# Stick-breaking and MoBA scores as two float32r products, a first stage of seven PSUM banks fed one block at a time, and a planner with leads by stage

## The chip, the cores and the metric

The kernel runs on one core of a Trainium2 chip. The metric is the device time of one launch in microseconds. Before the change it is 1304.44 us, the median of three runs (1304.07 to 1304.82).

## The reference

Two stacks of two layers each over 256 tokens of width 1024 (batch 1). A layer of the first stack computes a modulation vector from `c` (`silu(c) @ w_ada + b_ada`), normalises and modulates x, and multiplies by a wide `w_in` whose columns are split:

```python
hdn = modulate(rmsnorm(x, norm1_g[l]), shift1, scale1)
proj = hdn @ w_in[l]
q_lat, c_kv, k_pe, sb_qkv, mb_qkv, gates = jnp.split(proj, SPLIT_POINTS, axis=-1)
```

Three attentions with 8 heads follow. Multi-head latent attention (MLA) goes through the latents `q_lat` and `c_kv`; its heads have width 96. Stick-breaking attention (heads of width 64) takes a cumulative product of `sigmoid(-score)` in place of a softmax. MoBA (heads of width 64, rotary embedding on 16 columns) is at this length plain causal softmax. The three results are gated, projected, summed and added to x; then comes a squared-ReLU feed-forward of width 4096. A layer of the second stack (the first of them on 512 tokens, 256 of x and 256 of a context; the last on the 256 of x as queries) has softmax attention, a Fourier mixer, a pooling branch and a short convolution, each gated by a `silu` of its own columns and concatenated before an output projection.

## The kernel before, in words

The program is written as a recording. `record` (from line 499) runs the whole computation once against an object that notes every operation with its engine, its buffers and a modelled cost (`Recorder.cost`). `Scheduler` then orders the operations: `forward` places them greedily by priority on five engines, with a limited number of buffers (`SLOTS` and `CAPS`: 40 SBUF tiles of 128x1024, 11 of 128x544, and 8 PSUM banks in two classes, four "mm" and four "tr"); `backward` gives each operation its latest time, from which the next pass's priority is made after subtracting a lead. `LEAD` names a lead for eight kinds of work (`nc.part`), and the best of `PASSES` = 8 passes is kept. `emit` (line 447) issues the operations in that order, so every instruction of the profile carries the line of the one call in `emit`, L463. Tiles are told apart by their names.

Nearly all matrix products are products of float32r parts: an operand is split into a rounded part (`hi`, a cast on ScalarE) and the rest (`lo`, a subtraction on VectorE), and `mm3` (line 529) issues three matmuls, hi by hi, hi by lo and lo by hi. `wload` loads a weight tile and splits it (`raw`, `whi`, `wlo` in the profile). `gemm_tok` puts tokens on the PSUM partitions, `gemm_col` puts output columns there ("g" and "gc"). In the second stack, "cb" are the column products of the branches and `store_cat` (line 1403) splits each branch result into `cat`, with the subtraction on GpSimd.

The beginning is `lat_first` (line 1044). It loads x, normalises and transposes it ("nT_n"), and then goes in four steps of two blocks of 128 input rows: `ada_lead` loads the part of `w_ada` for the shift and scale of those two blocks (eight multiply-adds of 512 columns on VectorE, "acc"; then four one-column matmuls, "mT"), two normalised blocks are modulated and split into `hT0h` and `hT0l`, and 1312 columns of `w_in` are multiplied: the 1056 of the latents ("lat", six banks of 352 columns) and the first 256 of the stick-breaking queries ("latq"). Two of the three `lo` parts of the latents' weights are made on GpSimd.

The rest of `w_ada` and all of `w_mod_2` is multiplied by vectors on VectorE between other work: a generator (`filler`) hands out a quarter of a chunk at a time, at `RATE` per megabyte of weights loaded, or all at once when the result is needed.

Scores of stick-breaking and MoBA attention are plain float32 products in `causal_attention` (line 971). `to_q` (line 1038) copies the transposed queries into one of two tiles, `q_pad`, in which the other head's 64 partitions are zero, so that a product over 128 partitions with a `kT` tile that holds two heads gives one head's scores. For each attention and layer there are 16 such products, 8 with 128 key columns and 8 with 256 ("s_sb", "s_mb"). A float32 product appears in the trace as two matmul instructions.

```python
for i, h in enumerate(heads):
    mm(ps[:, i * nk:(i + 1) * nk], qT(h)[:, t * 128:(t + 1) * 128], kT(h)[:, 0:nk],
       start=(i == 0), stop=True)
```

Of the kernel before, what the change touches and what calls it, by code (L numbers as in the profile page):

```python
# [167 lines left out]
class Recorder:  # L168
    ENGINES = ("tensor", "vector", "scalar", "gpsimd", "sync")

    def __init__(self):
        self.protos = bacc.Bacc("TRN2", target_bir_lowering=False, num_devices=1)
        self.ops = []
        self.bufs = []
        self.masks = {}
        self.part = None
        self.group = None
        self.proto_of = {}
        for e in self.ENGINES:
            setattr(self, e, Engine(self, e))  # L180
# [311 lines left out]

VEC = (("norm1_g", 8), ("norm2_g", 8), ("b_ada", 48), ("q_norm_g", 6), ("kv_norm_g", 2),
# [3 lines left out]
def record(nc, a, out):  # L497
# [46 lines left out]
    vt = fixed([128, 24 + L * vn], F32, "vt")  # L544
    nc.sync.dma_start(out=vt, in_=a["vecs"])
    nc.sync.dma_start(out=ct[:, 0:128], in_=a["const_early"][:, 0:128])
    for t in range(2):
        nc.sync.dma_start(out=x[:, t], in_=a["x"][0, t * 128:(t + 1) * 128, :])
    x_late = nc.ops[-1]
    nc.sync.dma_start(out=ct[:, 128:cn], in_=a["const_early"][:, 128:cn])  # L550
    nc.order(x_late, nc.ops[-1])
# [11 lines left out]
    nc.vector.tensor_tensor(cT, vt[:, 0:24], cT, op=ALU.mult)  # L563

# [7 lines left out]
    def rope_tables():  # L572

        nc.sync.dma_start(out=pos_i, in_=a["positions"].rearrange("o (t p) -> p (o t)", p=128),
# [19 lines left out]

    rope_tables()
# [37 lines left out]
    def ada_raw(w2d, k, per, c0, count, n, name):  # L633
# [3 lines left out]
        for i in range(count):  # L637
            src = w2d[k * 128:(k + per) * 128, c0 + i * D:c0 + i * D + n]
            nc.sync.dma_start(out=view[:, :, i], in_=src.rearrange("(k p) n -> p k n", p=128))
            if first_weights:  # L640
                nc.order(first_weights[0], nc.ops[-1])
# [9 lines left out]
    def ada_chunk(w2d, c0, count, accs):  # L651
# [11 lines left out]
        for (_, fin), acc in zip(accs, tiles):  # L663
            fin(acc)
        yield

    def row_sum(acc, name):

        p = TR(f"rs{name}")
        with nc.together(87.0):  # L670
            for i in range(4):
                mm(p[32 * i:32 * i + 32, 0:256], ones_f, acc[:, i * 256:(i + 1) * 256])
        row = S2(f"rr{name}", 256)
        nc.scalar.copy(row, p[:, 0:256])
        turn = T([4, 256], F32, "dram", f"turn{name}")
        nc.sync.dma_start(out=turn, in_=row[0:128:32, :])
        return turn

    def ada_lead(w2d, key, bias, j):

        uid[0] += 1
        u = uid[0]
        acc = S2(f"acc{u}", 512)
        p = TR(f"mT{u}")
        for k in range(0, 8, 2):
            raw = ada_raw(w2d, k, 2, j * 256, 2, 256, f"araw{u}_{k}")
            for i in range(2):
                mul_add(acc, raw[:, i], 0, k + i)
        for b in range(4):
            mm(p[:, b:b + 1], acc[:, b * 128:(b + 1) * 128], ones_f[:, 0:1], start=(b == 0), stop=True)  # L690
        o = 2 * j
        nc.vector.tensor_tensor(modT[key].rearrange("p (i b) -> p i b", i=2)[:, :, o:o + 2],
                                p[:, 0:4].rearrange("p (i b) -> p i b", i=2),
                                bias.rearrange("p (i b) -> p i b", i=2)[:, :, o:o + 2], op=ALU.add)

    def fin_T(key, bias, q):

        def f(acc):
            nm = f"{uid[0]}_{key[0]}"
            turn = row_sum(acc, nm)  # L700
# [6 lines left out]
        return f  # L707

    def fin_bc(key, bias_row):

        def f(acc):
# [4 lines left out]
            turn = row_sum(acc, f"{uid[0]}_{key[0]}g")  # L716
            nc.sync.dma_start(out=g, in_=turn.rearrange("a n -> (a n)").partition_broadcast(128))
        return f
# [35 lines left out]
    def filler_step():  # L754
        try:
            next(filler[0][1])
        except StopIteration:
            filler.pop(0)

# [211 lines left out]
    def causal_attention(qT, kT, vf, scale, mask, act, name, rows, table=None):  # L971

        def probs(t, heads):
# [4 lines left out]
            for i, h in enumerate(heads):  # L978
                mm(ps[:, i * nk:(i + 1) * nk], qT(h)[:, t * 128:(t + 1) * 128], kT(h)[:, 0:nk],
                   start=(i == 0), stop=True)  # L980
# [51 lines left out]


    q_pad = [fixed([128, 4, 256], F32, f"q_pad{r}") for r in range(2)]
    for r in range(2):
        nc.gpsimd.memset(q_pad[r][64 - 64 * r:128 - 64 * r], 0.0)

    def to_q(b, p):

        for r in range(2):  # L1040
            nc.scalar.copy(q_pad[r][64 * r:64 * r + 64, b:b + 2], p[64 * r:64 * r + 64])


    def lat_first(w_in, g, act, evac, q0, q_evac):


        xT = [S4(f"xT{t}").rearrange("p (k t) -> p k t", k=8) for t in range(2)]
        for t in range(2):
            rr = rstd(sq_all(x[:, t], f"x0{t}"), D, f"n10{t}", EPS)
            xn = S4(f"xn_n10{t}")  # L1050
            nc.vector.tensor_scalar(xn, x[:, t], rr, math.sqrt(D), op0=ALU.mult, op1=ALU.mult)
            for k0 in (0, 4):
                p = TR(f"nT_n10{t}{k0}")
                for k in range(4):
                    nc.tensor.transpose(p[:, k * 128:(k + 1) * 128], xn[:, (k0 + k) * 128:(k0 + k + 1) * 128], ident)
                nc.scalar.copy(xT[t][:, k0:k0 + 4], p.rearrange("p (k t) -> p k t", k=4))
        key = ("a", 0, 0)
        modT[key] = fixed([128, 16], F32, "modT_a00")
        A = small(8, "A_n10")
        ps = {(t, c): (MM if c < 2 else TR)(f"lat{t}{c}") for c in range(3) for t in range(2)}  # L1060
        pq = TR("latq")
        last = None
        for k in range(0, 8, 2):
            i0 = len(nc.ops)
            nc.part = "lead"
            ada_lead(a["w_ada"][0], key, vec(0, "b_ada")[:, 0:16], k // 2)
            if last is not None:
                nc.order(last, next(op for op in nc.ops[i0:] if op.eng == "sync"))
            nc.vector.scalar_tensor_tensor(A[:, k:k + 2], modT[key][:, 8 + k:10 + k], 1.0, g[:, k:k + 2],
                                           op0=ALU.add, op1=ALU.mult)  # L1070
            for t in range(2):
                nt = S2(f"nt_n10{t}{k}", 256).rearrange("p (k t) -> p k t", k=2)
                for i in range(2):
                    nc.scalar.activation(nt[:, i], xT[t][:, k + i], AF.Identity, scale=A[:, k + i:k + i + 1],
                                         bias=modT[key][:, k + i:k + i + 1])
                for _, _, h, lo in act.spans(k, 2):
                    hv, lv = h[:, :, tok(t)], lo[:, :, tok(t)]
                    nc.scalar.copy(hv, nt)
                    nc.vector.tensor_tensor(lv, nt, hv.bitcast(F32), op=ALU.subtract)
            nc.part = None  # L1080
            i0 = len(nc.ops)
            ws = [wload(w_in, k * 128, 2, c * 352, 352, None if c == 0 else nc.gpsimd) for c in range(3)]
            wq = wload(w_in, k * 128, 2, q0, 256)
            last = [op for op in nc.ops[i0:] if op.eng == "sync" and op.bufs[0].kind == "r"][-1]
            for t in range(2):
                for c in range(3):
                    for i, (wh, wl) in enumerate(ws[c]):
# [633 lines left out]
```

## Time and profile before

| what | value |
|---|---|
| median of three runs | 1304.44 us |
| the profiled execution's own time | 1304.07 us |
| its span (first to last instruction) | 1302.3 us |
| mean granted TensorE clock | 0.997 of full |
| matmuls on TensorE | 1269.2 us busy, 97% |
| VectorE | 1027.5 us busy, 79% |
| ScalarE | 709.5 us busy, 54% |
| GpSimd | 135.5 us busy, 10% |
| moved by DMA | 272.67 MB, 209 GB/s over the span |

Matmuls are pipelined: one that is listed with 280 ns may start 118 ns after the one before. What a matmul costs TensorE is therefore read from the distance of two starts, not from its duration. A busy share of 97% does not say that nothing waits. The profile starts its clock at the first instruction, and the own time of an execution is 1.8 us longer than its span.

### The profile page before, as it was taken

How to read it: one execution, taken by the hardware profiler on the slowest of the kernel's cores; microseconds unless marked ns; L12 is line 12 of the kernel's file. 1: busy time of each engine (PE TensorE's matmuls, PEld its weight loads, DVE VectorE, ACT ScalarE, POOL GpSimd, SP SyncE). 2: the span in 40 equal slices, each digit the busy share in tenths (PEclk: the TensorE clock that was granted, in tenths of full speed). 3: DMA queues.
4: the chain of work that ended last, by engine and by line, in shares of the span. 5: the costliest groups of instructions: out<-in, count | busy, mean ns of one | idle time of the engine just before them, and what ended most of it. 6: DMA issues, size and time to landing. Idle time of an engine off the chain costs nothing.

```text
span 1302.3 us, 21802 instructions
## 1 busy us (share of the span) xinstructions
PE 1269.2 (97%) x8228; PEld 1119.8 (86%) x8228; DVE 1027.5 (79%) x1619; ACT 709.5 (54%) x1224; POOL 135.5 (10%) x142
## 2 busy tenths in 40 slices
PE   5999999999999999999999999999999999999998
PEld 4999989998898989999899988898878776788886
DVE  6898878977876667878687879987978868968874
ACT  5667656644655536566565545656555443326551
POOL 3300000110000000200000110000001033601232
PEclk9999999999999999999999999999999999999999
DMA  9987575665888667775755756897662326716530
GB/s 313 353 282 241 157 265 178 227 196 181 290 300 294 213 192 258 238 258 169 248 174 176 260 202 215 254 319 230 200 221 78 121 68 220 223 40 209 162 116 33
DMA packets 168031, 272.67 MB, mean 209 GB/s; under 512 B 26139, under 2 KB 65007, under 8 KB 167926
## 3 DMA queue, kind: packets, MB, share of 16 engines
q1 hardware_dynamic: 167926, 271.28, 62.8%
q8 instruction: 64, 1.05, 0.3%
q14 instruction: 41, 0.34, 0.1%
HBM read 270.11 MB, written 1.13 MB: 208 GB/s over the span
## 4 chain that ended last, share of the span: by engine, by line
PE 53%; DMA 3%; DVE 2%; issue 1%; ACT 1%; POOL 1%; SPq 0%; DVEq 0%; ACTq 0%; POOLq 0%
PE g L463 11%; PE gc L463 9%; PE cb L463 8%; PE ff L463 7%; PE f L463 7%; PE qkvp L463 2%; DMA raw<-w_in 1%; PE ufp L463 1%; POOL mean L463 1%; PE s_l L463 1%; PE pT_l L463 1%; PE pv L463 1%; PE s_ml L463 0%; PE s_mb L463 0%; DMA araw<-w_ada 0%
## 5 line engine op out<-in xcount | busy, mean ns | idle before, releaser
L463 ACT CAST whi<-raw 128x1024 fp32r<-128x1024 f32 (+3 forms) x370 | 368.8, 1012 | 254.3 <-DMA raw<-w_ff 66.2
L463 DVE TENSOR_TENSOR wlo<-raw,whi 128x1024 fp32r<-128x1024 f32 (+3 forms) x362 | 425.4, 1199 | 64.8 <-ACT whi L463 48.6
L463 DVE SCALAR_TENSOR_TENSOR acc<-araw,cT,acc 128x1024 f32<-128x1024 f32 (+1 forms) x175 | 211.6, 1226 | 23.0 <-DMA araw<-w_ada 18.2
L463 PE MATMUL gc<-hT1h,whi 128*128 128x256 f32 x256 | 78.8, 308 | 0.0
L463 PE MATMUL gc<-hT0h,whi 128*128 128x256 f32 x240 | 74.0, 308 | 0.0
L463 PE MATMUL gc<-hT1l,whi 128*128 128x256 f32 x256 | 72.0, 281 | 0.0
L463 PE MATMUL gc<-hT1h,wlo 128*128 128x256 f32 x256 | 72.0, 281 | 0.0
L463 PE MATMUL gc<-hT0h,wlo 128*128 128x256 f32 x240 | 67.5, 281 | 0.0
L463 PE MATMUL gc<-hT0l,whi 128*128 128x256 f32 x240 | 67.3, 281 | 0.0
L463 PE MATMUL f<-fT1h,whi 128*128 128x256 f32 x192 | 54.3, 283 | 0.0
L463 PE MATMUL f<-fT0h,whi 128*128 128x256 f32 x192 | 54.0, 281 | 0.0
L463 PE MATMUL f<-fT1l,whi 128*128 128x256 f32 x192 | 53.9, 281 | 0.0
L463 PE MATMUL f<-fT1h,wlo 128*128 128x256 f32 x192 | 53.9, 281 | 0.0
L463 PE MATMUL f<-fT0h,wlo 128*128 128x256 f32 x192 | 53.8, 280 | 0.0
L463 PE MATMUL f<-fT0l,whi 128*128 128x256 f32 x192 | 53.8, 280 | 0.0
L463 PE MATMUL cb<-h20h,whi 128*128 128x512 f32 x128 | 53.3, 417 | 0.0
L463 PE MATMUL cb<-h20h,wlo 128*128 128x512 f32 x128 | 51.0, 399 | 0.0
L463 PE MATMUL cb<-h20l,whi 128*128 128x512 f32 x128 | 51.0, 398 | 0.0
L463 PEld LDWEIGHTS gc<-hT1h,whi 128*128 128x128 f32 x256 | 48.3, 189 | 2.1 <-issue 1.3
L463 PEld LDWEIGHTS gc<-hT1l,whi 128*128 128x128 f32 x256 | 48.5, 190 | 0.5
L463 PEld LDWEIGHTS gc<-hT1h,wlo 128*128 128x128 f32 x256 | 48.4, 189 | 0.0
L463 PEld LDWEIGHTS gc<-hT0h,whi 128*128 128x128 f32 x240 | 45.3, 189 | 2.7 <-issue 2.1
(639 smaller groups left out, 3720.0 us busy)
## 6 DMA issues: line engine op xcount, KB each, us to landing
raw<-w_in SPq DMA_DIRECT2D x138, 512.0 KB, 4.9
raw<-w_ff SPq DMA_DIRECT2D x128, 512.0 KB, 5.1
araw<-w_ada SPq DMA_DIRECT2D x128, 256.0 KB, 4.8
araw<-w_ada SPq DMA_DIRECT2D x32, 512.0 KB, 4.4
raw<-w_out SPq DMA_DIRECT2D x32, 512.0 KB, 5.3
araw<-w_mod SPq DMA_DIRECT2D x64, 256.0 KB, 4.6
raw<-w_in SPq DMA_DIRECT2D x24, 352.0 KB, 6.5
araw<-w_mod SPq DMA_DIRECT2D x16, 512.0 KB, 5.4
```

The source lines that it names most:

```text
L463: op.inst.append(getattr(getattr(nc, op.eng), fn)(*[val(x) for x in args], **{k: val(x) for k, x in kw.items()}))
```

## The change: what it does

It has several parts.

- Scores: queries and keys of stick-breaking and MoBA are kept as float32r. A tile of queries holds a head's rounded part on its own 64 partitions and the rest on the other 64; the tile of keys holds the rounded keys on both halves, and a second tile `k_low` the rest of the keys on the head's half and zeros on the other. Two products over 128 partitions give hi by hi plus lo by hi, and hi by lo. MLA scores stay float32.
- First stage: `lead_first` takes the place of `lat_first`. It goes block by block (eight steps of 128 input rows), with `w_ada` and `w_in` columns laid out for it ahead of the launch, and fills seven banks of 512: the 512 query, 512 key and 512 value columns of stick-breaking and 256 gate columns, 1792 in all. For the first two blocks the modulation is multiplied on TensorE (32-column stationary tiles, "c_col"), for the other six on VectorE in pieces of 256 columns. The latents come afterwards by `gemm_tok`. All `lo` parts of its weights are made on VectorE. Rotary tables are made after it, and the order of the first loads changes.
- Filler: where one chunk serves two vectors (second stack), the sums of both go through one bank and one copy.
- `kpe` (MLA): one transpose of a padded tile in place of two. Pool branch: the matmuls of both halves are issued together.
- `store_cat`: the subtraction moves from GpSimd to VectorE.
- Planner: a lead for each of some 35 stages is added to the lead by kind, the leads by kind are changed, `PASSES` is 3 in place of 8 and `RATE` 0.4354 in place of 0.428.

```diff
-            op.lead = 0.0 if eng == "sync" else LEAD.get(self.part, 0.0)
+            op.lead = 0.0 if eng == "sync" else LEAD.get(self.part, 0.0) + LEAD.get(self.stage, 0.0)
...
-    q_pad = [fixed([128, 4, 256], F32, f"q_pad{r}") for r in range(2)]
+    k_low = [fixed([128, 4, 256], F32R, f"k_low{r}") for r in range(2)]
...
+        def to_q(self, b, p):
+            for r in range(2):
+                own, other = (slice(64 * i, 64 * i + 64) for i in (r, 1 - r))
+                hi = self.q[r][own, b:b + 2]
+                nc.scalar.copy(hi, p[own])
+                nc.vector.tensor_tensor(self.q[r][other, b:b + 2], p[own], hi.bitcast(F32), op=ALU.subtract)
+
+        def to_k(self, b, p):
+            for r in range(2):
+                own, other = (slice(64 * i, 64 * i + 64) for i in (r, 1 - r))
+                hi = self.k[r][own, b:b + 2]
+                nc.scalar.copy(hi, p[own])
+                nc.vector.tensor_tensor(k_low[r][own, b:b + 2], p[own], hi.bitcast(F32), op=ALU.subtract)
+                nc.scalar.copy(self.k[r][other, b:b + 2], p[own])
+
+        def scores(self, o, h, t, nk, first):
+            q, r = self.q[h % 2][:, h // 2, t * 128:(t + 1) * 128], h % 2
+            mm(o, q, self.k[r][:, h // 2, 0:nk], start=first, stop=False)
+            mm(o, q, k_low[r][:, h // 2, 0:nk], start=False)
...
+        for k in range(8):
+            nc.part = "lead"
+            acc = S2(f"acc_l{k}", 256)
...
+            raws = [load(a["lead_ada"][k, :, i * 1024:(i + 1) * 1024], 1024, f"araw_l{k}{i}") for i in range(2)]
...
+            if k < LEAD_ROWS:
+                r = TR(f"mR_l{k}")
+                for i in range(2):
+                    with nc.together(87.0):
+                        for q in range(4):
+                            mm(r[32 * q:32 * q + 32, 0:256], c_col[:, 4 * i + q], raws[i][:, q * 256:(q + 1) * 256],
+                               start=(i == 0), stop=(i == 1))
+                nc.scalar.copy(acc, r[:, 0:256])
+            else:
+                for q in range(8):
+                    mul_add(acc, raws[q // 4][:, (q % 4) * 256:(q % 4 + 1) * 256], 0, q)
...
+            nt = S2(f"nt_n10{k}", 256)
+            for o in (act.h(k), nt):
+                nc.scalar.activation(o, xT[k // 4][:, k % 4], AF.Identity, scale=A[:, k:k + 1], bias=mod[:, 0, k:k + 1])
+            nc.vector.tensor_tensor(act.l(k), nt, act.h(k).bitcast(F32), op=ALU.subtract)
...
+                nc.scalar.copy(hi[:, 0:n], raw)
+                nc.vector.tensor_tensor(lo[:, 0:n], raw, hi[:, 0:n].bitcast(F32), op=ALU.subtract)
...
+            lead_first(vec(0, "norm1_g"), hT,
+                       [(0, "col", put_q(0)), (256, "col", put_q(1)), (512, "col", put_k(0)), (768, "col", put_k(1)),
+                        (1536, "col", lambda p: nc.scalar.activation(gt_lead[:, 0:512], p, AF.Tanh, scale=0.5)),
+                        (1024, 0, put_v(0)), (1024, 1, put_v(1))])
+            rope_tables()
...
-            nc.gpsimd.tensor_tensor(cat.l(kb)[:, sl], c, h.bitcast(F32), op=ALU.subtract)
+            nc.vector.tensor_tensor(cat.l(kb)[:, sl], c, h.bitcast(F32), op=ALU.subtract)
...
-PASSES = 8
-RATE = 0.428
-LEAD = {"norm": 2550.0, "lead": 2700.0, "residual": -2030.0, "sb": -4670.0, "ml": -11260.0, "mb": -7380.0,
-        "attention2": -8540.0}
+PASSES = 3
+RATE = 0.4354
+LEAD = {"norm": 2550.0, "lead": 2700.0, "lead weights": 2950.0, "residual": -1660.0, "sb": -8810.0, "ml": -16600.0,
+        "mb": -6240.0, "attention2": -17800.0, "ada": 3060.0, "att mb0": -190.0, "att mb1": -1340.0,
...
```

## Rows read from the trace of the kernel before

**Rows 1.** The page: TensorE's and VectorE's busy time; the chain's shares by engine.

```profile
PE 1269.2 (97%) x8228; PEld 1119.8 (86%) x8228; DVE 1027.5 (79%) x1619; ACT 709.5 (54%) x1224; POOL 135.5 (10%) x142
...
PE 53%; DMA 3%; DVE 2%; issue 1%; ACT 1%; POOL 1%; SPq 0%; DVEq 0%; ACTq 0%; POOLq 0%
```

**Rows 2.** Windows of 50 us: busy of each engine, clock, DMA share, GB/s.

```profile
0.00:50.00 50.00, 32.84 (x180) 30.14 (x181) 36.78 (x57) 24.57 (x47) 17.38 (x21) 0.97 0.97 316
...
800.00:850.00 50.00, 50.00 (x331) 44.64 (x330) 48.72 (x47) 27.89 (x35) 0.00 (x0) 1.00 0.85 274
...
1050.00:1100.00 50.00, 47.58 (x257) 34.72 (x256) 37.78 (x65) 18.61 (x47) 18.29 (x19) 0.97 0.41 136
...
1200.00:1250.00 50.00, 47.18 (x363) 42.52 (x363) 41.59 (x78) 26.48 (x49) 12.64 (x17) 1.00 0.47 154
1250.00:1300.00 50.00, 46.98 (x304) 38.70 (x302) 29.31 (x52) 17.12 (x37) 12.98 (x14) 1.00 0.21 70
sum 1300.00, PE 1269.17 PEld 1119.76 DVE 1027.53 ACT 709.46 POOL 135.52; mean PE 48.81 PEld 43.07 DVE 39.52 ACT 27.29 POOL 5.21
```

**Rows 3.** Timeline of TensorE in the first stage: start, duration, what, count.

```profile
19.27 0.66 PE L463 MATMUL lat<-whi,hT0h 128*128 128x352 f32 x1 [0.42 <-ACT hT0h L463]
...
48.35 1.02 PE L463 MATMUL mT<-ones_f,acc 128*128 128x1 f32 x8
...
58.65 0.28 PE L463 MATMUL latq<-hT0h,whi 128*128 128x256 f32 x1
58.76 0.28 PE L463 MATMUL latq<-hT0l,whi 128*128 128x256 f32 x1
...
60.08 0.28 PE L463 MATMUL gc<-hT0h,whi 128*128 128x256 f32 x1
```

**Rows 4.** Groups of VectorE instructions by form, mostly to 60 us: count, busy, mean ns.

```profile
L463 DVE SCALAR_TENSOR_TENSOR acc<-araw,cT,acc 128x512 f32<-128x512 f32 x28 | 22.3, 798 | 0.8
L463 DVE TENSOR_TENSOR hT0l<-nt_n,hT0h 128x256 fp32r<-128x256 f32 x8 | 4.0, 516 | 0.7 <-ACT hT0h L463 0.6
L463 DVE TENSOR_TENSOR wlo<-raw,whi 128x1024 fp32r<-128x1024 f32 x3 | 3.7, 1223 | 1.0 <-PE lat L463 0.7 <-ACT whi L463 0.3
L463 DVE TENSOR_TENSOR wlo<-raw,whi 128x704 fp32r<-128x704 f32 x4 | 3.5, 878 | 0.0
...
L463 DVE SCALAR_TENSOR_TENSOR A_n<-modT_a,vt 128x2 f32<-128x2 f32 x16 | 4.7, 325 | 0.3
```

**Rows 5.** One tile's instructions (s_mb) and TensorE's timeline around them.

```profile
L463 PE MATMUL s_mb<-kTmb,q_pad x64: 270/326/382, 216.7 to 710.8; 128*128 128x128 f32 x32, 128*128 128x256 f32 x32
...
216.69 0.61 PE L463 MATMUL s_mb<-kTmb,q_pad 128*128 128x128 f32 x4
217.06 0.36 PE L463 MATMUL gc<-hT0h,whi 128*128 128x256 f32 x1
217.26 0.28 PE L463 MATMUL gc<-hT0l,whi 128*128 128x256 f32 x1
...
709.36 0.59 PE L463 MATMUL s_mb<-kTmb,q_pad 128*128 128x256 f32 x2
709.60 0.47 PE L463 MATMUL gc<-oml1h,whi 128*128 128x256 f32 x1
709.90 0.28 PE L463 MATMUL gc<-oml1l,whi 128*128 128x256 f32 x1
```

**Rows 6.** Copies of queries out of PSUM; a VectorE operation that reads PSUM.

```profile
L463 ACT COPY q_pad<-gc x6: 581/582/587, 66.0 to 532.6; 64x512 f32<-64x512 f32 x6
...
L463 DVE TENSOR_TENSOR rt_o<-g,gate_a 128x512 f32<-128x512 f32 x8 | 5.5, 689 | 3.3 <-PE g L463 3.3
```

**Rows 7.** The chain that ended last, near the end: start, length, what.

```profile
1274.48 1.21 POOL cat1l L463
...
1277.63 2.62 POOL cat1l L463 x2
```

**Rows 8.** Timeline at 1076 us, VectorE and TensorE: who waits for what.

```profile
1076.71 1.99 DVE L463 SCALAR_TENSOR_TENSOR acc<-araw,cT,acc 128x1024 f32<-128x1024 f32 x1 [2.29 <-DMA araw<-w_mod]
...
1082.81 0.41 PE L463 MATMUL pT_l<-ct,p_l 128*128 128x128 f32 x2 [1.91 <-DVE p_l L463]
```

More of the change, by code (lines that the diff above doesn't have):

```diff
@@ L176, in __init__ @@
         self.part = None
+        self.stage = None
         self.group = None
@@ L490, in spans @@
             k += m
+LEAD_RANGES = ((1056, 2592), (5152, 5408))
+LEAD_ROWS = 2
+LEAD_COLS = sum(e - s for s, e in LEAD_RANGES)
 VEC = (("norm1_g", 8), ("norm2_g", 8), ("b_ada", 48), ("q_norm_g", 6), ("kv_norm_g", 2),
@@ L544, in record @@
     vt = fixed([128, 24 + L * vn], F32, "vt")
+    nc.sync.dma_start(out=x[:, 0], in_=a["x"][0, 0:128, :])
     nc.sync.dma_start(out=vt, in_=a["vecs"])
     nc.sync.dma_start(out=ct[:, 0:128], in_=a["const_early"][:, 0:128])
[L547 to L551, printed above, removed]
+    nc.sync.dma_start(out=x[:, 1], in_=a["x"][0, 128:256, :])
     pos_i = fixed([128, 2], I32, "pos_i")
@@ L715, in f, with after @@
             nc.vector.tensor_tensor(acc[0:1, :], acc[0:1, :], g[0:1, :], op=ALU.add)
-            turn = row_sum(acc, f"{uid[0]}_{key[0]}g")
-            nc.sync.dma_start(out=g, in_=turn.rearrange("a n -> (a n)").partition_broadcast(128))
-        return f
+        def after(turn):
+            nc.sync.dma_start(out=gate_bc[key], in_=turn.rearrange("a n -> (a n)").partition_broadcast(128))
+        return before, after
     def ada_first(l, part):
@@ L758, in filler_step @@
             filler.pop(0)
+        nc.stage = stage
     def filler_tick(n):
@@ L1057, in lat_first @@
         key = ("a", 0, 0)
         modT[key] = fixed([128, 16], F32, "modT_a00")
+        mod = modT[key].rearrange("p (i b) -> p i b", i=2)
+        bias = vec(0, "b_ada")[:, 0:16].rearrange("p (i b) -> p i b", i=2)
         A = small(8, "A_n10")
[L1060 to L1063, printed above, removed]
-            i0 = len(nc.ops)
[L1065 to L1069, printed above, removed]
-                                           op0=ALU.add, op1=ALU.mult)
[L1071 to L1079, printed above, removed]
-            nc.part = None
[L1081 to L1087, printed above, removed]
-                        mm3(ps[t, c][:, 0:352], act.h(k + i)[:, tok(t)], act.l(k + i)[:, tok(t)], wh, wl,
-                            k + i == 0, k + i == 7)
-            for i, (wh, wl) in enumerate(wq):
-                for m in range(2):
-                    c = slice(m * 128, (m + 1) * 128)
-                    mm3(pq[:, m * 256:(m + 1) * 256], wh[:, c], wl[:, c], act.h(k + i), act.l(k + i),
-                        k + i == 0 and m == 0, k + i == 7)
@@ L1097, in lat_first @@
+        first_weights.extend(last)
         rate[0] = RATE
-        for t in range(2):
-            for c in range(3):
-                evac(t, ps[t, c][:, 0:352], c)
     def first_layer(l, ss1, after_ff):
@@ L1332, in first_layer @@
             ff2(g - 2, hid[g - 2])
+        nc.stage = f"ff end{l}"
         res = after_ff(ss)
@@ L1522, in second_layer @@
             store_cat(m, zf[:, m], p[:, 0:W])
+        nc.stage = f"pool{l}"
         ups = []
```

237 lines of the change are left out of this document (157 added, 80 removed), and 6 rows, old and new, of the table LEAD.

## The prediction, made before the change was run

> **What bounds the kernel now.** I read the page first. TensorE has matmuls in flight for 97% of the span, no other engine reaches 80%, and the chain that ended last is mostly TensorE, with DMA, VectorE, ScalarE, GpSimd and issue time at 8% together, about 104 us [rows 1]. So TensorE is the bound, and a change pays if it takes matmul time away, puts matmuls where TensorE now waits, or removes a wait. Then the windows of 50 us: the idle time over the run is 1300 - 1269.2 = 30.8 us, of which 17.2 lie in the first 50 us; 2.4, 2.8 and 3.0 us lie in the stretches 1050 to 1100 and 1200 to 1300 (the second stack's attention and the end), and only some 5.4 us in everything else [rows 2]. Waits shorter than a matmul's own latency are not in that sum, since pipelined matmuls overlap them. Last, the price of a matmul: two starts of 256 columns of float32r are 0.118 us apart within a run of twelve [rows 3].
>
> The sum is made against the profiled execution's own 1304.1 us, which lies 0.4 us under the median of the runs; I make no correction for that. What a measurement of this kernel can tell from no change is about 0.2%, 2.6 us.
>
> **First stage.** In the kernel before, the first weight matmul starts at 19.3 us and the stage ends at 60.1 us, where the next product follows without a gap [rows 3]. It covers 1312 columns; the new one covers 1792. The 480 columns more are 3.75 groups of 128, times 8 blocks, times 3 matmuls at 0.118 us: 10.6 us of TensorE that no longer follow the stage. What counts is when the new stage ends.
>
> Its loads: x 1.05 MB, constants and vectors 0.2 MB, eight times 1.05 MB of modulation weights and 0.92 MB of projection weights, together 17 MB; at the 316 GB/s of the first 50 us [rows 2] that is 54 us. TensorE needs 7 banks x 6 x 0.118 = 5.0 us a block, 40 us, so it can follow. VectorE is the tighter one. A block from the third on has eight multiply-adds of 256 columns. From the two widths of the weight subtraction a column costs (1223 - 878) / 320 = 1.08 ns, so the 798 ns of 512 columns become 0.52 us at 256 [rows 4]; eight are 4.1 us. To that come the weight subtractions of 1024 and 768 columns, 1.22 and 0.95 us, the activation's, 0.5, and two tiny ones at up to 0.33 us [rows 4]: 7.2 us a block with some overlap, 43 us for six blocks. The third block's first modulation weights land after 5.4 MB, at 17 us. So VectorE is done at 60 us and TensorE, with the last block's seven banks behind it, at 65: 5 us later than now. Net 10.6 - 5.2, I take **-5 us**. Ends: -11 if VectorE is not what limits and the stage ends where it ends now, +4 if each block loses 1 us more to the chain from modulation over ScalarE to TensorE. The two blocks whose modulation goes through TensorE cost it some 2 us while it waits anyway. The rotary tables and the later first loads lie under this stage and cost nothing; without that cover, they would meet the latents' products, which follow.
>
> [...]
>
> **Scores.** Each of two attentions in two layers has 8 products of 128 key columns and 8 of 256, and each float32 product is two instructions [rows 5]. The pair with 256 columns costs 709.90 - 709.36 - 0.118 = 0.42 us, the pair with 128 (217.26 - 216.69 - 0.118) / 2 = 0.23 us [rows 5]. After the change a product is two float32r matmuls. With 256 columns that is 2 x 0.118 = 0.24 us: 32 x 0.19 = 6 us less. No row shows float32r with 128 moving columns. The nearest is a float32 matmul of a single column, 8 in 1.02 us, 0.11 to 0.13 us each [rows 3]: loading 128 stationary columns seems to set a floor. By it two matmuls cost 0.22 us, what the pair costs now, and I take 0 for these. Ends: 0.059 each, half of a 256-column one, gives 3.5 us more; if float32r at 128 columns costs what float32 does, 7 us are lost. **-6 us**, from -9.5 to +1.
>
> [...]
>
> **What the scores need.** A pair of head groups now takes, for queries, two copies on ScalarE and two subtractions on VectorE, and for keys four and two. Over four projections with four evacuations each, that is 24 copies more at 0.58 us on ScalarE, 14 us, and 32 subtractions from PSUM at 0.69 us on VectorE, 22 us [rows 6]. They lie beside TensorE, which has gate and value columns to multiply meanwhile; ScalarE is busy half the time. A PSUM bank is held some 2 us longer at the keys. I cost it at **0**, with an end of +6 where the cover is gone; late next would be the first scores of each attention.
>
> **store_cat.** Near the end the chain goes through GpSimd's subtractions for 1.21 and 2.62 us [rows 7]. On VectorE one of 256 columns is at most 0.52 us [rows 4], two 1.0: **-3 us**, since TensorE's last products stand behind them; from -4 to +2, if VectorE has older work in its queue. In the first layer of the second stack it costs VectorE 6 us that it has there.
>
> **Small ones, 0 together.** The filler's sums have as many matmuls as before, one copy and one bank less where there are two vectors; the transposes of `kpe` are two fewer over the run; the pool matmuls wait for the later of two halves, within 1 us either way.
>
> **Order.** Leads by stage change the order everywhere. The waits of rows 2 outside the first stage are 13.6 us, and those of the second stack come from order: VectorE stands 2.3 us behind a load of filler weights, and TensorE then waits 1.9 us for a softmax row [rows 8]. The filler has its own lead now, and the attention of the second stack a much larger one. I take **-9 us** (8 of visible idle, less the 3 already counted, and 4 of waits inside busy time). The ends are wide, as no row prices an order: -30, under a third of the chain's 104 us, and +12.
>
> Sum: -5 - 6 + 0 - 3 - 9 = -23, so **1281 us**.
>
> **Rivals.** *Order gives much more*: the waits hidden in busy time come out as well, -25 to -30 in place of -9: 1260 to 1265. For it: 104 us of the chain are not TensorE's. Against it: 13.6 us only are visible. *The gains don't arrive*: the new first stage ends 10 us later than the old, so that its columns are paid again, or the order loses about as much as it wins: 1288 to 1300. For it: six blocks of 7.2 us on a VectorE with nothing to spare. *VectorE becomes the bound*, slower: it gets 22 us for the heads, 8 x 0.88 = 7 us of latent weights that GpSimd now has, and 10 us of `store_cat`, 39 us in all. If they all lengthen the way, 1281 + 39 = 1320 us. It decides where VectorE nears 98% of a stretch. Against it: at 800 to 850 us it is busy for 48.7 of 50 us and TensorE does not idle [rows 2], and over the run it has 20% left. *float32r at 128 columns costs as much as float32*: 7 us less gain, 1288.
>
> **Chances.** Forecast (1268 to 1288) 0.42; more from the order (1250 to 1268) 0.27; gains that don't arrive, with the dear 128 columns (1288 to 1302) 0.20; VectorE as the bound or an order that loses more than all the gains (over 1307) 0.08; in between, within 0.2%, 0.03. So faster by over 0.2% is 0.89, within 0.2% 0.03, slower 0.08. The range from 1256 to 1299 leaves out the 0.08 and 0.03 above, and some 0.07 below.
>
> **What would show it.** The first stage: its last matmul at 63 to 68 us, VectorE without gaps from 17 us on, and the latents' products behind it without a wait. Scores: starts 0.118 us apart at 256 columns and about 0.11 at 128; 0.06 or 0.23 there proves the floor wrong. The end: no GpSimd in the last 30 us of the chain. Order: less than 10 us of TensorE idle after the first stage. The forecast is wrong if VectorE's busy share passes 90% over stretches in which TensorE idles, or if the first stage ends after 72 us.

## The result, and the profile after

The changed kernel takes 1312.41 us (1312.01 to 1313.49, 4 runs) against 1304.26 us beside it. The ratio is 1.0068, with a 95% interval of 1.0056 to 1.0080: 0.7% slower. Forecast were 1281 us, in a range from 1256 to 1299.

The profiled execution has a span of 1310.1 us, an own time of 1312.1 us and a mean granted clock of 0.991. The page's busy times, to be held against [rows 1]:

```profile
PE 1270.7 (97%) x8258; PEld 1116.8 (85%) x8258; DVE 1044.5 (80%) x1705; ACT 727.0 (55%) x1246; POOL 85.0 (6%) x112
```

TensorE is in flight as long as before, although the scores are cheaper (a pair of 256 columns takes 0.23 us where it took 0.42, e13 below). The windows tell where the time is. First two wide ones of the kernel before, the second up to its last matmul; its short ones are [rows 2] (columns: busy of TensorE, its weight loads, VectorE, ScalarE and GpSimd, then the granted clock, the DMA share and GB/s):

```profile
0.00:150.00 150.00, 132.20 (x929) 124.61 (x930) 125.63 (x205) 98.11 (x171) 26.18 (x36) 0.99 0.84 280
...
150.00:1298.00 1148.00, 1136.97 (x7301) 995.15 (x7300) 900.52 (x1413) 611.35 (x1054) 109.33 (x106) 1.00 0.61 201
```

The same two of the changed kernel, and then its short ones up to 150 us:

```profile
0.00:150.00 150.00, 127.95 (x876) 116.13 (x877) 116.63 (x231) 98.70 (x169) 8.50 (x28) 0.94 0.73 251
...
150.00:1305.80 1155.80, 1142.71 (x7384) 1000.63 (x7383) 926.51 (x1473) 628.25 (x1078) 76.50 (x84) 1.00 0.61 203
...
0.00:50.00 50.00, 37.49 (x253) 30.46 (x253) 31.48 (x68) 29.42 (x46) 4.86 (x17) 0.97 0.90 311
50.00:100.00 50.00, 43.89 (x269) 41.92 (x267) 40.34 (x79) 36.27 (x70) 1.16 (x2) 0.93 0.80 275
100.00:150.00 50.00, 46.57 (x356) 43.75 (x357) 44.80 (x86) 33.02 (x54) 2.48 (x10) 0.94 0.50 167
```

Two things are to be seen. From 150 us to the last matmul the visible idle time of TensorE is 11.0 us before (1148.0 - 1136.97) and 13.1 after (1155.8 - 1142.71): the new order took none of it away. In the first 150 us it grew from 17.80 to 22.05 us, and the granted clock fell: 0.03, 0.07 and 0.06 of 50 us are 8.0 us of lost clock, 6.5 more than before (0.03 of 50 us there). Another 1.5 us are lost at 1000 to 1050 (granted 0.97), as before at 1050 to 1100 [rows 2].

The place is in TensorE's timeline of the changed kernel (start, duration, what, count; in brackets the idle time before it and who ended it):

```profile
57.72 0.39 PE L464 MATMUL ld<-hT0h,whi_l 128*128 128x256 f32 x1 [1.66 <-ACT hT0h L464]
58.67 0.58 PE L464 MATMUL ld<-hT0l,whi_l 128*128 128x256 f32 x1 [0.57 <-DVE hT0l L464]
...
62.46 0.41 PE L464 MATMUL ld<-hT0h,wlo_l 128*128 128x256 f32 x1
62.68 0.41 PE L464 MATMUL ld<-hT0h,whi_l 128*128 128x256 f32 x1
...
71.77 0.39 PE L464 MATMUL ld<-whi_l,hT0l 128*128 128x512 f32 x1
72.00 0.32 PE L464 MATMUL g<-whi,hT0h 128*128 128x352 f32 x1
...
96.08 0.28 PE L464 MATMUL s_sb<-kssb,qssb 128*128 128x128 f32 x1
96.19 0.28 PE L464 MATMUL s_sb<-k_low,qssb 128*128 128x128 f32 x1
100.04 1.51 PE L464 MATMUL nT_ql<-ct,xn_ql 128*128 128x128 f32 x6 [3.57 <-DVE ssv_ql L464]
102.35 1.47 PE L464 MATMUL nT_kvl<-ct,xn_kvl 128*128 128x128 f32 x4 [0.79 <-DVE nt_ql L464]
103.47 0.67 PE L464 MATMUL g<-whi,laT0h 128*128 128x384 f32 x1
```

The first stage ("ld") ends at 72.0 us, not 65. It waits 2.2 us at 57 to 59, and after that 256-column matmuls start 0.21 us apart (granted clock 0.57 and 0.58 in the windows of the last section, 0.50 in those of 2 us from 60 to 64); from 67 to 70 us, at a granted clock of 1.00, they start 0.118 us apart, as in [rows 3]. Behind the latents' products ("g", 72.0 to 95.5) TensorE waits 4.4 us for their norm, and the granted clock is 0.50 from 100 to 106 us. In the kernel before, the same transposes had no wait, because products of queries and keys stood around them, and the up projection began at 90.2:

```profile
73.52 0.28 PE L463 MATMUL gc<-hT0h,wlo 128*128 128x256 f32 x1
73.63 0.49 PE L463 MATMUL nT_ql<-ct,xn_ql 128*128 128x128 f32 x3
73.88 0.37 PE L463 MATMUL gc<-hT0h,whi 128*128 128x256 f32 x1
...
90.19 0.44 PE L463 MATMUL g<-whi,laT0h 128*128 128x384 f32 x1
```

It now begins at 103.47, 13.3 us later. By then 256 gate columns (2 x 8 x 3 matmuls at 0.118, 5.7 us) and eight score matmuls (0.8 us) more are done, so 6.8 us are lost. From the start of the up projection to the end the changed kernel takes 1206.6 us; before it takes 1212.1, of which 6.5 are those matmuls. So the rest of the run, where scores, `store_cat` and order were to bring 18 us, is 1.0 us longer for the same work.

### The profile page after: what moved, and what is told of

Its sections match the earlier page's. It is cut to its first block, busy times and chain, and to the rows that moved or that the text cites. A ratio compares the mean times of both kernels' runs of the same rounds, so it can differ in the third digit from the quotient of the medians.

```text
span 1310.1 us, 21962 instructions
## 1 busy us (share of the span) xinstructions
PE 1270.7 (97%) x8258; PEld 1116.8 (85%) x8258; DVE 1044.5 (80%) x1705; ACT 727.0 (55%) x1246; POOL 85.0 (6%) x112
## 5 line engine op out<-in xcount | busy, mean ns | idle before, releaser
L464 ACT CAST whi<-raw 128x1024 fp32r<-128x1024 f32 (+3 forms) x354 | 351.8, 1014 | 247.3 <-DMA raw<-w_ff 44.0
L464 DVE TENSOR_TENSOR wlo<-raw,whi 128x1024 fp32r<-128x1024 f32 (+3 forms) x354 | 412.5, 1195 | 38.3 <-ACT whi L464 33.1
L464 DVE SCALAR_TENSOR_TENSOR acc<-araw,cT,acc 128x1024 f32<-128x1024 f32 x147 | 190.2, 1313 | 37.8 <-DMA araw<-w_ada 26.5
L464 PE MATMUL gc<-hT1h,whi 128*128 128x256 f32 x256 | 74.0, 289 | 0.0
L464 PE MATMUL gc<-hT0h,whi 128*128 128x256 f32 x176 | 51.7, 294 | 0.0
L464 PE MATMUL gc<-hT0l,whi 128*128 128x256 f32 x176 | 49.4, 281 | 0.0
L464 PE MATMUL gc<-hT0h,wlo 128*128 128x256 f32 x176 | 49.3, 280 | 0.0
L464 PE MATMUL g<-whi,hT1h 128*128 128x512 f32 (+1 forms) x112 | 43.4, 388 | 0.0
```

Of the source, the lines that this page charges most:

```text
L464: op.inst.append(getattr(getattr(nc, op.eng), fn)(*[val(x) for x in args], **{k: val(x) for k, x in kw.items()}))
```

## The experiments

Three theories stood at the start. **Theory 1**: the new first stage takes away the products that covered the latents' norm, and what was put under the stage stalls VectorE. **Theory 2**: the new leads and the order made from them lose the time over the whole run. **Theory 3**: the extra copies and subtractions for the scores' low parts lose it. Ratios are to the kernel before on the same chip, which had medians from 1303.2 to 1303.8 us.

| run | median us | ratio, 95% interval |
|---|---|---|
| e1 rotary tables later | 1311.2 | 1.0069 (1.0044 to 1.0094) |
| e2 as e1, one gap filled | 1310.1 | 1.0057 (1.0039 to 1.0074) |
| e3 scores alone | 1307.7 | 1.0032 (1.0020 to 1.0043) |
| e4 old leads | 1317.3 | 1.0100 (1.0084 to 1.0117) |
| e5 old first stage | 1312.8 | 1.0072 (1.0059 to 1.0085) |
| e6 float32 scores | 1306.6 | 1.0022 (1.0013 to 1.0031) |
| e7 four rows | 1317.7 | 1.0111 (1.0098 to 1.0124) |
| e8 before, new draw | 1307.2 | 1.0032 (1.0020 to 1.0044) |
| e9 one attention in float32 | 1306.7 | 1.0020 (1.0010 to 1.0031) |
| e10 no extra operations | 1311.4 | 1.0063 (1.0050 to 1.0076) |
| e11 after, new draw | 1308.0 | 1.0037 (1.0023 to 1.0052) |
| e12 store_cat on GpSimd | 1312.8 | 1.0063 (1.0043 to 1.0084) |
| e13 before, float32r scores, same order | 1299.6 | 0.9970 (0.9958 to 0.9982) |
| e14 after, float32 scores, same order | 1313.3 | 1.0087 (1.0064 to 1.0111) |
| e15 three gaps filled | 1308.3 | 1.0047 (1.0030 to 1.0064) |
| e16 before, second draw | 1303.9 | 1.0005 (0.9994 to 1.0015) |
| e17 scores alone, second draw | 1307.1 | 1.0023 (1.0011 to 1.0035) |
| e18 scores alone, third draw | 1303.3 | 0.9997 (0.9988 to 1.0005) |

**The stage and its cover: e1, e5, e7.** In the changed kernel VectorE waits inside the stage for `pos_i`, which is loaded behind all of the stage's weights, with the eighth block's multiply-adds queued behind it:

```profile
56.40 0.17 DVE L464 CAST posf<-pos_i 128x2 f32<-128x2 int32 x1 [1.27 <-DMA pos_i<-positions]
```

e1 moves the tables' VectorE operations behind that, after the planner has run, so that all other operations keep their order:

```diff
+    for i, op in enumerate(rec.rope):
+        if op.eng == "vector" and op.start < max(heads):
+            op.start = max(heads) + 0.01 * (i + 1)
```

> The changed kernel in its own order, except that VectorE's operations of the rotary tables stand behind the seventh first-stage bank's first evacuation and no longer in the middle of the stage. Theory 1 (the cover of the first stage is gone and what was put under it stalls VectorE): the wait of 1.3 us for pos_i and the following 0.4 us tables leave the stage, TensorE does not idle 1.7 us there and the clock does not fall for 6.8 us, so the last first-stage matmul starts at 66 to 69 us in place of 71.8 and the time is 1306 to 1309, ratio to the kernel before 1.002 to 1.005. Theory 2 (the planner's new leads and order lose the time over the whole run): first stage shorter perhaps, but the time stays at 1311 to 1313. Theory 3 (the heads' extra copies and subtractions lose it): no change, 1312.

The last matmul of the stage starts at 70.3 us and the time is the same. TensorE still waits at 57 us, for ScalarE and VectorE in turn, and the clock still falls (0.50 from 60 to 62 us). Timeline of TensorE in e1:

```profile
57.73 0.39 PE L464 MATMUL ld<-hT0h,whi_l 128*128 128x256 f32 x1 [0.92 <-ACT hT0h L464]
58.68 0.39 PE L464 MATMUL ld<-hT0l,whi_l 128*128 128x256 f32 x1 [0.56 <-DVE hT0l L464]
```

So the wait for `pos_i` is not the cause of the loss. e5 puts the whole first stage back:

```diff
-            lead_first(vec(0, "norm1_g"), hT, ...)
+            lat_first(w_in, vec(0, "norm1_g"), hT, lat_evac, 1056, lambda p: hd_sb.to_q(0, p))
```

> The changed kernel with the first stage of the kernel before (1056 latent columns and 256 of the queries, two blocks at a time, rotary tables and loads in the old places); float32r scores, the leads by stage and all the rest stay. Theory 1 (the new first stage and what it leaves uncovered loses the time): the stage ends at 60 us again, the latents' norm chain lies beside the products of queries, keys and values, and the loss of 15 us between 50 and 150 us is gone, while the 10.6 us of columns are paid after the stage: 1299 to 1305, ratio 0.996 to 1.001. Theory 2 (the order by the new leads): 1308 or more.

Nothing came back, so the new stage by itself is not what loses the time, and theory 1 alone fails. Planned under the new leads, the old stage ends at 65.1 us and not at 60.1: before it, the normalised x comes late, and inside it the activation's low part waits longer (3.3 us in the kernel before, and from 10 us on nothing for the first). In all TensorE waits 13.9 us from 10 to 66 us in e5, and 8.6 from 10 to 60 in the kernel before. The two longest in e5 (us in total, times, longest):

```profile
PE nT_n L464 <- DVE xn_n L464: 3.9, 1, 3.9
PE lat L464 <- DVE hT0l L464: 5.6, 3, 2.5
```

e7 asks what sets the stage's end, VectorE or the loads (`LEAD_ROWS = 4`).

> The changed kernel with LEAD_ROWS 4: the modulation of four blocks, not two, goes through TensorE, so VectorE has 8.2 us less in the first stage and TensorE some 2.2 us more. If VectorE sets the end of the stage: last first-stage matmul at 66 to 69 us, time 1307 to 1310. If the loads set it: last one at 70 to 72 us, 1311 to 1314. In both, the wait of the latents' transposes behind the stage stays.

The last first-stage matmul starts at 70.8 us: with two blocks' modulation taken from VectorE the stage ends 1.0 us earlier, and the kernel is slower by 5 us. In this order, then, VectorE's multiply-adds are not what the stage ends with. A hold-up of the loads is to be seen: between 19 and 24 us the DMA queue of the changed kernel stands 4.6 us until first-stage products free a buffer. That it sets the stage's end was not tried.

**The leads: e4.** The leads, passes and rate of the kernel before, in the changed kernel.

> The changed kernel planned with the leads, the eight passes and the filler rate of the kernel before (the stages' names stay, without leads). Theory 2 (the new leads and three passes lose the time): 1300 to 1306. Theory 1: the loss from 50 to 150 us stays, as does the gain of the scores, and the order is no better elsewhere: 1310 to 1322, with a first stage that ends at 70 us or later.

It is slower by another 4 us by the ratio: the old leads don't bring the time back, and theory 2 in this form fails. That the new leads suit the changed kernel better is not shown by it, as a new order alone moves the time as much (e8 and e11 below).

**The clock: e2, e15.** e2 is e1 with 30 matmuls of 256 columns into a bank that is overwritten next, ahead of the latents' transposes. e15 has 22 there, 10 in the first stage ahead of the seventh block and 10 ahead of the second stack's first output product:

```diff
+        op.calls = [("matmul", (o, h[:, 0:128], h), kw)] * n + op.calls
```

> As e1, and 30 matmuls of 256 columns whose result is not used fill the gap of TensorE ahead of the latents' transposes (4.4 us of waits at 98 to 103 us). Theory 1: the gap's idle time stays, but the second stretch of half clock (6.8 us, at about 98 to 106 us) goes or shrinks, 2 to 3.4 us less than e1, 1303 to 1307. If the clock there costs nothing, because what follows waits for VectorE anyway: as e1, or up to 2 us more, since the fill may end later than the data come.

> The changed kernel in its own order with VectorE's rotary tables behind the first stage (as e1), and unused matmuls in three waits of TensorE: 10 in the first stage ahead of the seventh block, 22 ahead of the latents' transposes, 10 ahead of the first product of the second stack's output. If the half clock after these waits costs its face value (9.5 us of clock by the windows, of which 3 are also in the kernel before): 1304 to 1307, with a mean clock of 0.998 or more. If only the waits themselves cost: 1309 to 1312.

e2 shows little by itself: its clock is 0.998, its time 1 us under e1's with wide intervals, and its 30 matmuls end behind the data they wait for. In e15 the clock stays up from 50 to 150 us. Windows of e15, and the start of its transposes:

```profile
50.00:100.00 50.00, 46.78 (x311) 43.99 (x311) 43.47 (x88) 39.12 (x75) 2.50 (x4) 1.00 0.83 284
100.00:150.00 50.00, 47.79 (x387) 45.35 (x387) 46.65 (x80) 34.76 (x56) 1.15 (x7) 1.00 0.52 168
```

```profile
97.26 0.82 PE L464 MATMUL nT_ql<-ct,xn_ql 128*128 128x128 f32 x6
```

The time is 1308.3, between the two expectations: against e1 some 3 us less (0.0022 of 1303.5), but the intervals overlap, so this alone doesn't show a gain. Other runs bear on it. e12 and e14 (below) keep the changed kernel's order and fill nothing. In their profiles the stage has much the same waits, but the clock stays at 1.00 from 50 to 75 us (0.86 in the changed kernel), and the stage ends at 69.2 and 68.5 us in place of 72.0. TensorE's timeline in e14:

```profile
57.02 0.39 PE L464 MATMUL ld<-hT0h,whi_l 128*128 128x256 f32 x1 [1.62 <-ACT hT0h L464]
57.97 0.39 PE L464 MATMUL ld<-hT0l,whi_l 128*128 128x256 f32 x1 [0.56 <-DVE hT0l L464]
...
68.51 0.32 PE L464 MATMUL g<-whi,hT0h 128*128 128x352 f32 x1
```

So the lower clock costs the stage some 3 us where it comes, and the fill isn't shown to be what kept it away there; the transposes, 2.8 us earlier in e15 than in the changed kernel, start at 97.1 in e12 too. Behind the second wait only the filled kernels are at 1.00 from 90 to 112 us (e2, e15; 0.84 in the changed kernel, e1, e10 and e12, 0.92 in e14). Over all 42 executions of the seven kernels with this order, an execution with 0.001 more of granted clock than its kernel's mean took 0.7 to 1.0 us less, though the four of the changed kernel don't show it (0.991: 1312.0 and 1312.1 us; 0.995: 1312.7 and 1313.5). About 3 of the 8 us for the clock is therefore an estimate, less than the 6.5 of the windows, and not shown by one experiment.

**Extra operations: e10, e12.** e10 turns the low parts' subtractions and the keys' second copies into memsets on GpSimd, in the planned order.

```diff
+    for op in rec.extra:
+        op.eng = "gpsimd"
+        op.calls = [("memset", (op.calls[0][1][0].bitcast(F32), 0.0), {})]
```

> The changed kernel in its own planned order; the subtractions for the low parts and the second copies of the keys (32 on VectorE, 16 on ScalarE) are replaced by memsets to zero on GpSimd at the same places, so the scores lack their low parts. Theory 3 (the copies and subtractions delay what follows): the waits behind the first stage (4.4 us at 100 to 103) and at the first softmax rows shrink, 1303 to 1308. If the order or the first stage itself is the cause: 1310 to 1313.

It is 1 us faster by the medians, and by the intervals not more than 3: theory 3 fails as the main cause. The run's trace suggests why the latents' norm is late without these operations too. In the changed kernel the filler's loads (`araw`) stand in SP's queue for 13.3 us. For 12.6 of them they wait for VectorE, up to `rope_s`, an operation of the rotary tables, and a weights' subtraction beside it at 79.4 us; these stand behind the heads' subtractions, so the tables did not stay under the stage. Four of the six loads of the up projection's weights (`w_uq`) leave behind them at 82 us, and ScalarE, which casts them ahead of the latents' last copies, waits 3.2 us for them. SP's timeline and its wait from 66 to 80 us, then ScalarE's waits from 84 to 98 us:

```profile
66.48 13.27 SPq L464 DMA_DIRECT2D araw<-w_ada  x2
82.16 3.25 SPq L464 DMA_DIRECT2D raw<-w_uq  x4
```

```profile
SPq L464 <- DVE rope_s L464: 12.6, 1, 12.6
```

```profile
ACT whi L464 <- DMA raw<-w_uq: 3.2, 3, 1.7
```

In e10, without the heads' subtractions, the filler's loads take 7.1 us, but `w_uq` leaves no earlier, since SP then waits 8.1 us for a latents' product to free a buffer, and TensorE waits nearly as long (3.1 and 0.8 us). SP's and TensorE's timelines in e10:

```profile
66.53 7.12 SPq L465 DMA_DIRECT2D araw<-w_ada  x2
81.80 3.25 SPq L465 DMA_DIRECT2D raw<-w_uq  x4
```

```profile
99.22 1.39 PE L465 MATMUL nT_ql<-ct,xn_ql 128*128 128x128 f32 x6 [3.11 <-DVE ssv_ql L465]
```

In the kernel before, these loads left from 59 to 69 us (SP's timeline):

```profile
59.29 1.73 SPq L463 DMA_DIRECT2D raw<-w_uq  x2
...
68.65 1.43 SPq L463 DMA_DIRECT2D raw<-w_uq  x2
```

e12 puts `store_cat`'s subtraction back on GpSimd, order kept (`op.eng = "gpsimd"`).

> The changed kernel in its own order, with the subtractions of store_cat on GpSimd again. If the predicted gain of 3 us of that move is there: 1314 to 1317. If they lie under TensorE's work now: 1311 to 1313. If VectorE is what the second stack waits for: 1308 to 1311.

The same time (1.0063 against 1.0068): the move is worth nothing that can be measured, and a gain of 3 us lies just outside the intervals.

**The scores, order free: e3, e6, e9.** e3 puts float32r scores into the kernel before (its `to_q`, `to_k` and `scores` as in the change). e6 puts float32 scores into the changed kernel, e9 does so in the first layer's stick-breaking attention alone.

```diff
-            hd_sb, (v_sb, vf_sb) = Heads("sb0"), values("sb")
+            hd_sb, (v_sb, vf_sb) = Heads32("sb0"), values("sb")
```

> The kernel before with one part of the change: float32r scores with stacked high and low parts, the old leads, old first stage and old placement of everything else (the planner orders it anew). Theory 1: the scores' 6 us are gained without a new wait, 1297 to 1300, ratio 0.994 to 0.997. Theory 3: the extra copies and subtractions eat the gain, 1303 to 1312. A new order of the planner may add or take 2 us either way.

> The changed kernel with float32 scores and the old copies of queries and keys (one subtraction and one copy fewer per group); new first stage, new leads. Theory 1 and 2: the 6 us of the scores are lost, 1316 to 1320. Theory 3 (extra copies and subtractions delay): 1306 to 1311. A new order by the planner may move it by up to 4 us either way.

> The changed kernel with float32 scores and plain copies in one of its four attentions, the stick-breaking one of the first layer, whose queries and keys leave their banks right behind the first stage; the other three keep float32r. If the extra copies and subtractions of that one attention cause the loss (they stand on ScalarE and VectorE ahead of the latents' casts and norm): first stage ends at 65 to 68 us, the waits at 96 to 103 us shrink below 2 us, the scores' gain of the other three stays, 1300 to 1305. If each attention loses about as much by its copies as it wins: 1309 to 1312. If it is the planner's scatter alone: anywhere from 1304 to 1316, without these two signs.

All three point the wrong way: the scores cost 4 us in e3, and giving them up in four attentions or in one gains 6 us. In e6's profile the first stage ends at 65.8 us, as the prediction had it, and the norm is hardly waited for (0.5 us, and 1.4 more ahead of the up projection; TensorE's timeline in e6):

```profile
65.78 0.32 PE L464 MATMUL g<-whi,hT0h 128*128 128x352 f32 x1
...
90.39 0.85 PE L464 MATMUL nT_ql<-ct,xn_ql 128*128 128x128 f32 x6 [0.46 <-DVE ssv_ql L464]
```

But each of these kernels was also planned anew, as were e4, e5 and e7; the next two sets separate the two.

**The draw of the order: e8, e11, e16.** The same instructions, placed anew because the filler's rate differs by 0.1 to 0.2%: 0.427 and 0.429 in the kernel before, 0.4358 in the changed one.

> The kernel before with the filler's rate at 0.427 in place of 0.428: the same instructions, placed anew by the planner. If small moves in the planner's order are worth several microseconds (which would explain why float32r scores alone gave 1307.7): off by 2 to 6 us from 1303.5 either way. If the order scatters little: 1302 to 1305, and the loss with the scores alone is then theirs.

> The changed kernel with the filler's rate at 0.4358 in place of 0.4354: the same instructions, placed anew. If the planner's scatter explains why float32 scores were faster by 6 us: off by 3 to 7 us from 1312 either way. If the scatter is small here: 1310 to 1315, and the 6 us belong to the scores' copies.

> The kernel before with the filler's rate at 0.429, a second new draw of its order. If its own order is a lucky one: 1306 to 1310, as e8. If e8 was the unlucky one: 1302 to 1305.

A new draw moved the kernel before by +4 and by 0 us, and the changed one by -4. That is nearly as much as any of the effects above, so e3, e6 and e9 say little about the scores by themselves, and the few us of e4, e5 and e7 against the changed kernel little about their parts.

**The scores, order fixed: e13, e14.** The planner runs as it did; afterwards the scores' operations alone are exchanged.

```diff
+            if fn == "matmul" and args[1].buf in heads:
+                calls.append((fn, args, dict(kw, stop=False)))
+                calls.append((fn, args, dict(kw, start=False)))
```

> The kernel before in its own planned order on every engine; queries and keys of stick-breaking and MoBA attention are rounded to float32r and each score is two float32r matmuls of them in place of one float32 product, so the low parts are missing (and the scores doubled). Only TensorE's time for the scores changes. If the scores' time is on the path: 6 us less, 1296 to 1299. If it is hidden behind waits that grow by as much: 1302 to 1304.

> The changed kernel in its own planned order, scores as one float32 product of the unrounded queries and keys (the low parts are then zero, their subtractions and copies stay). The mirror of e13. If the scores' time is on the path: 5 to 7 us more, 1317 to 1320. If hidden: 1310 to 1314. If the order and not the arithmetic made e6 faster, this is not below 1310.

e13 is 0.30% faster (0.18 to 0.42%), 4 us: most of the forecast 6 arrive when nothing is moved. The pair of 256 columns takes 0.23 us where it took 0.42 [rows 5], counted as in the prediction: from its start to the second start behind it, less 0.118. TensorE's timeline in e13:

```profile
706.40 0.40 PE L463 MATMUL s_mb<-kTmb,q_pad 128*128 128x256 f32 x2
706.64 0.28 PE L463 MATMUL gc<-oml1h,whi 128*128 128x256 f32 x1
706.75 0.28 PE L463 MATMUL gc<-oml1l,whi 128*128 128x256 f32 x1
```

e14 lies 0.0019 above the changed kernel, 2.5 us, with intervals that overlap. That fits scores whose time lies in part, perhaps all, under other waits in this order; the intervals don't exclude the full 6 us either.

**The scores alone, two more draws: e17, e18** (rates 0.429 and 0.425).

> As e3 (the kernel before with float32r scores, high and low part stacked, the old first stage and leads), planned with the filler's rate at 0.429. If e3's 1307.7 was an unlucky draw: 1298 to 1303. If the longer evacuations and the three more buffers cost the gain in any order: 1304 to 1309.

> As e17, with the rate at 0.425. The same two expectations: 1298 to 1303 if e3 was an unlucky draw, 1304 to 1309 if the gain is lost in any order.

With e3, the scores alone have 1307.7, 1307.1 and 1303.3 us, 1306.0 in the mean; the kernel before has 1303.6, 1307.2 and 1303.9, 1304.9 in the mean. Stacked scores planned anew give no gain that three draws show, and none of these draws beats the kernel before clear of noise. e13, which does, leaves the low parts out; with them the heads need three more buffers of 4 KB per partition than the kernel before has, so its order can't be kept, and that version wasn't tried.

## Why the prediction was wrong

The sum said -23 us and the runs +8, 31 us apart. Some 12 of them stand ahead of the up projection, where the first stage was to give -5 and the kernel is 6.8 us late; 19 stand behind it, where scores, `store_cat` and order were to give -18 and the work takes 1.0 us more.

*Order, -9, is the step that failed by most.* It was read from idle time that one order had, as if another would not have its own; of its 13.6 us, 2.0 (1298 to 1300) even lie behind the last matmul. Visible idle from 150 us to the last matmul went from 11.0 to 13.1 us, and e8, e11 and e16 show that the draw alone moves the time by 0 to 4 us. The ends of -30 to +12 held that; the value taken, 8 of 13.6 us, rested on nothing but the hope that waits go where leads change.

*First stage, -5.* Loads and banks were sized right: the last block's weights reached ScalarE at 54.7 us (54 forecast). The stage ended at 72.0 all the same, 11.9 us later than before, for 10.6 us of columns. The sum let the last blocks follow one another without a wait and had no term for the clock; the waits of 2.2 us at 57 us and the 3.4 us of clock behind them (0.43 and 0.42 of 4 us, last section) are most of the 7 us by which the stage ends late. Where the same order kept its clock (e12, e14), it was 3.5 to 4 us late. That VectorE is without gaps from 17 us on was wrong too: it waits 2.6 us for ScalarE's normalised blocks, 1.3 for `pos_i`, 0.9 for TensorE and 0.9 for loads, the chain from modulation over ScalarE to TensorE that the +4 end was meant for. Its own pieces were even cheaper than the 0.52 us taken, 0.484 (groups of VectorE to 75 us):

```profile
L464 DVE SCALAR_TENSOR_TENSOR acc_l<-araw_l,cT,acc_l 128x256 f32<-128x256 f32 x42 | 20.3, 484 | 0.9 <-DMA araw_l<-lead_ada 0.2
L464 DVE TENSOR_TENSOR hT0l<-nt_n,hT0h 128x256 fp32r<-128x256 f32 x8 | 3.4, 424 | 2.6 <-ACT nt_n L464 2.6
```

The prediction's own sign of being wrong, a first stage that ends after 72 us, named the right row.

*"They would meet the latents' products" was the warning, and stopped one step short.* What lost its cover is the latents' norm: 4.4 us of waiting and a second stretch at a granted clock of 0.50 (100 to 106 us), together most of the 6.8 us by which the up projection is late. The sum had no term for it, nor for the clock, for which some 3 us are estimated. That the late `w_uq` loads and the buffers they wait for cause the norm's delay is read from the queues of three kernels; no run gave the kernel more buffers, so it is not shown by experiment.

*Scores, -6: right as TensorE's time.* Starts are 0.118 us apart at 256 columns (from 67 to 70 us) and 0.11 at 128 (96.08 to 96.19 in the rows above), so the floor that the prediction put on a short matmul holds; that loading the stationary columns makes it is not shown. Of the 6 us, 4 reach the end in the kernel before with the order fixed (e13); in the changed kernel it is open whether any do (e14). The rival with the dear 128 columns is out.

*Heads' copies, 0: right* as far as e10 tells (1 us, at most 3). *store_cat, -3: wrong*, 0 by e12. GpSimd is gone from the chain's last 30 us as forecast, but the time did not follow it; the chain of the changed kernel ends in TensorE's products alone (start, length, what):

```profile
1276.98 6.53 PE cb L464 x54
1283.51 22.29 PE g L464 x96
```

The output products follow column products, not `store_cat`.

*The slower rival* named VectorE as the bound at 98% of a stretch. It is not: VectorE is at 80% over the run and at 78% in the first 150 us. The kernel got slower by another way, which no rival had: as its trace reads, a chain of small steps that lost the products around it, and no gain behind it. The chance of 0.08 for slower was too small, since a term that only an order gives (-9) carried two fifths of the gain.

What stays open: how the 8 us divide. e11's order of the same work is 4 us faster, some 3 us are estimated for the clock after the waits, and the two overlap; three orders of the kernel before lie at 1303.6 to 1307.2 us, two of the changed one at 1308.0 and 1312.4, too few to say what the edit costs in the mean. Which buffers would have to be free for the norm to be early is not settled, nor why the scores' gain doesn't show behind the up projection.

## What to carry to other kernels

Where a planner orders the work, an edit is priced twice: with the order kept, which shows what the edit itself gives, and over several draws, which show how much the order scatters; a single planned kernel of each kind can't tell a gain of 4 us from a draw. Before a product is moved ahead, ask which small chain it covered where it stood, and what stands there afterwards. A gap of a few microseconds in TensorE's work is to be counted with the clock that may be lost behind it: here 1.7 us of clock behind a wait of 2.4 us, 3.4 behind 2.2, and none behind another (next section).

## What was not expected of the hardware

After some short waits the granted clock was lower, at 0.72 in the kernel before, at 0.57 and 0.50 in the changed one. Windows of the kernel before around its wait of 2.4 us at 31 to 33 us (0.97 over the 50 us, [rows 2]), and then of the changed kernel around the waits at 57 and 100 us and a third one:

```profile
30.00:34.00 4.00, 1.62 (x9) 1.32 (x8) 3.93 (x6) 1.65 (x4) 0.89 (x1) 0.86 1.06 368
34.00:38.00 4.00, 4.00 (x20) 4.00 (x19) 3.69 (x6) 2.01 (x3) 0.45 (x1) 0.72 0.86 289
```

```profile
58.00:62.00 4.00, 3.43 (x17) 3.34 (x16) 3.16 (x9) 2.96 (x5) 0.00 (x0) 0.57 1.05 370
62.00:66.00 4.00, 4.00 (x21) 3.96 (x21) 3.90 (x10) 3.15 (x5) 0.00 (x0) 0.58 1.04 396
...
104.00:106.00 2.00, 2.00 (x9) 1.90 (x8) 1.80 (x5) 1.21 (x2) 0.00 (x0) 0.50 0.00 0
...
1140.00:1145.00 5.00, 2.66 (x12) 1.86 (x10) 5.00 (x5) 3.08 (x4) 0.00 (x0) 1.00 0.92 320
1145.00:1150.00 5.00, 4.84 (x21) 4.00 (x22) 4.89 (x8) 2.80 (x4) 0.00 (x0) 1.00 0.47 169
```

A wait of 2.4 us was followed by 1.7 us of lost clock in the kernel before, waits of 2.2 us by 3.4 in the changed one, and the wait at 1142 us by none; the same waits in the stage (1.62 and 0.56 us) were followed by none in e14. So the size of the loss can't be read from the wait. With matmuls that compute nothing in the gaps, the clock was at 1.00 from 50 to 150 us in e15; in the stage it was so in e14 without them, and behind the norm only with them.
